# MLP up-projection of a hybrid encoder block as seven block products (Strassen) with 256-column moving tiles

## The chip, the cores and the metric

One core of one Trainium2 chip runs the whole block in one launch. The metric is device time in microseconds, from the first to the last instruction of an execution; lower is better. Engines are named as in the profile: PE (matmul), PEld (its weight loads), DVE, ACT, POOL, SP (which issues nearly all DMAs).

## What is computed

One layer with 512 tokens of width 2048. The change touches one product in its second half:

```
h  = x + W_out( sig(gA) * P_A(NAtt(xn)) + sig(gB) * P_B(BiGDN(xn)) ),  xn = RMSNorm(x)
h  = h + W_down( relu(RMSNorm(h) W_up)^2 )        # W_up 2048 x 8192, W_down 8192 x 2048
y  = RMSNorm_final(h)
```

All data are float32. Tokens stand on the free axis (T = 512), channels on the 128 partitions, so the product with W_up has 64 output tiles of 128 channels, each summed over 16 tiles of 128 input channels.

## The kernel before

**Precision by splitting.** A matmul takes rounded operands (float32r). Each operand is therefore kept as a high half, a rounded copy made on ACT (`S_.copy`, L89 and L94), and a low half, what the rounding lost, made on DVE by a subtraction (L90 and L95). A product of two tiles is three matmuls, high by high, high by low and low by high (L115 to L117, `unit_mm`), each with a weight load of its own.

**Weights.** W_up lies in DRAM as units `wup[m, u]` of 128 x 1024 floats (512 KB): output tile m, half u of the input channels, eight 128 x 128 blocks. `load_unit` (L85) loads one (tag `raw`, four buffers), casts it (`wh`, three buffers) and subtracts (`wl`, three buffers). One unit feeds 24 matmuls.

**Stages at the change.** Around it the kernel runs, one after the other on PE:

- L795 to L815: the projections of both branches and their gated sum `mix`, 32 tiles (high and low) in the pool `bp` (tag `B`, 48 buffers of 128 x 512).
- L849 to L864: W_out, 16 output tiles of 48 matmuls. Each result is added to x (L855), stored to `hTD` for later (L856), scaled by the norm's weights and split into `hh[m]`, `hl[m]` (L861, L862). The first eight pairs go to `bp`, the other eight to the pool `hq` on the right-hand side of memory (L858, L860). `sumsq` gathers squares for the norm.
- L865: the task `stat("h")` makes the row of reciprocal roots `rB`. Tasks advance when `pump()` is called inside `unit_mm`, every four channel tiles; it puts some tiny matmuls between the others.
- L867 to L874: the up-projection. For each m of 64, 2 x 24 matmuls of 512 columns into one bank; u = 0 reads `hh[0..7]`, u = 1 reads `hh[8..15]`. DVE applies relu and `rB` (L872), ACT squares (L873), SP stores to `hidD[m]` (L874).
- L875, L876: while m >= 40, eleven of the first sixteen hidden tiles are already loaded back and split (`load_hid`, L841).
- L878 to L896: the down-projection in four blocks of 16 hidden tiles, added into `Ha` (loaded from `hTD` at L882); its last two output tiles are done in halves of 256 columns (L918 to L934), 192 matmuls.

PSUM holds seven banks for these stages (L785) and one for statistics. Pools on the right-hand side form a stack: one that is opened after another was closed gets the same place, and with `reuse_waits="tile"` a tile waits for just those tiles that it overwrites.

**What sets the order.** The text gives priorities and dependencies. When the program is built, a list scheduler picks for each engine the ready instruction of highest priority, so an engine's order is not that of the text, but it is fixed from then on, and each engine and each DMA queue runs its own list in order, waiting where a semaphore isn't there yet.

```
def unit_mm(ps, unit, rhs, k0, first, last, view=None):
    hi, lo = unit
    for kk in range(8):
        rh, rl = rhs[k0 + kk]
        w = slice(kk * 128, (kk + 1) * 128)
        PE.matmul(ps, hi[:, w], rh, start=first and kk == 0, stop=False)
        PE.matmul(ps, hi[:, w], rl, start=False, stop=False)
        PE.matmul(ps, lo[:, w], rh, start=False, stop=last and kk == 7)
```

Of the kernel before, what the change touches and what calls it, by code (L numbers as in the profile page):

```python
# [19 lines left out]
T = 512  # L20
# [7 lines left out]
NPUMP = 4  # L28
# [21 lines left out]
def tile_hybrid_block(  # L50
# [17 lines left out]
    nlw_s = cp.tile([128, KX], F32, name="nlw_s")  # L68
# [5 lines left out]
    def big(name, dt=F32R):  # L74
        return bp.tile([128, T], dt, tag="B", name=name)

    def ev(name):
        return st.tile([128, T], F32, tag="ev", name=name, bufs=4)

    def load_raw(src, name):  # L80
        raw = st.tile([128, 1024], F32, tag="raw", name=f"raw_{name}", bufs=4)
        nc.sync.dma_start(out=raw, in_=src)
        return raw

    def load_unit(src, name):  # L85
# [15 lines left out]
    def pump():  # L101
        for t in list(tasks):
            try:
                next(t)
            except StopIteration:
                tasks.remove(t)
# [5 lines that stand above are left out]
            if view is not None:  # L112
                rh, rl = view(rh), view(rl)
# [4 lines that stand above are left out]
            if kk % NPUMP == NPUMP - 1:  # L118
                pump()
# [31 lines left out]
    rB = cp.tile([128, T], F32, tag="rB", name="rB")  # L151
# [24 lines left out]
    hidD = dp.tile([64, 128, T], F32, name="hidD")  # L176
# [4 lines left out]
    X = []  # L181
    with ExitStack() as p0:
# [128 lines left out]
        for r in (127, 0):  # L311
            t = dn.tile([128, 128], F32, name=f"sel{r}")
# [411 lines left out]
        i = 3  # L724
# [40 lines left out]
        for h in range(NH):  # L765
            qkv = []
            for e, kind in enumerate(("aq", "ak", "av")):
                ps = mtile((kind, h), perm)
                t = ap.tile([128, T], F32, tag=kind, name=f"{kind}{h}", bufs=1 if e < 2 else 2)
# [5 lines left out]
            t = att_task(h, *qkv, ap)  # L775
# [8 lines left out]
    with ExitStack() as p1:  # L784
# [3 lines left out]
        def bank():  # L788
            return mmp.tile([128, T], F32, tag="mm", name="ps_b")

        mix = []
        with ExitStack() as p4:
# [3 lines left out]
            for h in range(NH):  # L796
                raw = ev(f"ybr{h}")
# [43 lines left out]
        def load_hid(k):  # L841
            raw = ev(f"hr{k}")
            nc.sync.dma_start(out=raw, in_=hidD[k])
            return split(raw, big(f"hih{k}"), big(f"hil{k}"))

        hT = []
        with ExitStack() as p5:
            hq = p5.enter_context(tc.tile_pool(name="hq", bufs=1, side="right", reuse_waits="tile"))
            for m in range(16):  # L849
                ps = bank()  # L850
                xr = ev(f"xr{m}")
                nc.sync.dma_start(out=xr, in_=xT[:, m, :])
                for u in range(2):
                    unit_mm(ps, load_unit(wout[m, u], f"wo{m}_{u}"), mix, 8 * u, u == 0, u == 1)
                V.tensor_tensor(out=xr, in0=ps, in1=xr, op=ALU.add)  # L855
                nc.sync.dma_start(out=hTD[m], in_=xr)  # L856
                if m < 8:
                    hh, hl = big(f"hh{m}"), big(f"hl{m}")  # L858
                else:
                    hh, hl = hq.tile([128, T], F32R, name=f"hh{m}"), hq.tile([128, T], F32R, name=f"hl{m}")  # L860
                S_.activation(out=hh, in_=xr, func=AF.Copy, scale=nlw_s[:, m : m + 1])  # L861
                V.scalar_tensor_tensor(out=hl, in0=xr, scalar=nlw_s[:, m : m + 1], in1=hh.bitcast(F32), op0=ALU.mult, op1=ALU.subtract)  # L862
                hT.append((hh, hl))
                sq = sumsq(xr, m, f"h{m}")  # L864
            tasks.append(stat("h", sq))  # L865
            hid0 = []
            for m in range(64):  # L867
                ps = bank()
                for u in range(2):
                    unit_mm(ps, load_unit(wup[m, u], f"up{m}_{u}"), hT, 8 * u, u == 0, u == 1)  # L870
                r = ev(f"ur{m}")
                V.scalar_tensor_tensor(out=r, in0=ps, scalar=0.0, in1=rB, op0=ALU.max, op1=ALU.mult)  # L872
                S_.activation(out=r, in_=r, func=AF.Square)  # L873
                nc.sync.dma_start(out=hidD[m], in_=r)  # L874
                if m >= 40 and m % 2 == 1 and len(hid0) < 11:  # L875
                    hid0.append(load_hid(len(hid0)))  # L876

        hp = p1.enter_context(tc.tile_pool(name="hp", bufs=1, side="right", reuse_waits="tile"))  # L878
        Ha = hp.tile([128, 16, T], F32, name="Ha")
# [4 lines left out]
        for b in range(NB):  # L884
# [4 lines left out]
            for m in range(14 if last else 16):  # L889
                ps = bank()  # L890
# [22 lines left out]
        for m in (14, 15):  # L913
            for u in range(2):
                raw = load_raw(wdn[m, 2 * NB - 2 + u], f"dnl{m}_{u}")
                for e in range(2):
                    pieces[m, 2 * u + e] = split(raw[:, e * T : (e + 1) * T], big(f"wlh{m}{u}{e}"), big(f"wll{m}{u}{e}"))
        for half in range(2):  # L918
            ts = slice(half * 256, half * 256 + 256)
            for m in (14, 15):  # L920
                ps = bank()[:, 0:256]
                for k in range(16):
                    wh, wl = pieces[m, k // 4]
                    w = slice(k % 4 * 128, k % 4 * 128 + 128)
# [7 lines left out]
                sq = sumsq(H[m], m, f"f{m}_{half}", ts)  # L932
# [88 lines left out]
```

## Time and profile before

| | us |
|---|---|
| median of 2 runs | 2957.06 |
| lowest, highest run | 2955.55, 2958.57 |
| profiled execution: span | 2960.0 |
| of it W_out (from the first to the last start) | 1360.36 to 1534.23 |
| of it the up-projection | 1534.46 to 2244.15 |
| PE busy | 2913.1 |
| DVE busy | 1365.7 |
| ACT busy | 872.6 |

The profiled execution is given by its span; no other time stands on its page. A busy time counts an engine's instructions from their start to their (for matmuls modelled) end. Matmuls overlap, so the distance between their starts tells what one costs PE. "Idle before" is the time that the engine sat idle ahead of a group of instructions, with what ended it.

### The profile page before, as it was taken

Reading aid. Unit: us, or ns where it says so; the run is one execution under the profiler, and the core shown is the slowest. Engines: PE = TensorE matmul, PEld = TensorE weight load, DVE = VectorE, ACT = ScalarE, POOL = GpSimd, SP = SyncE. Lnnn points to the kernel's source line nnn. Section 1 sums busy time; section 2 is a strip of 40 time slices with the busy share of each in tenths; the row PEclk is TensorE's granted clock in tenths of the full one; section 3 lists DMA queues with packets and bytes.
Section 4 is the critical chain, followed back from the end, with each engine's and each line's share of the span. In section 5 each row is a group of like instructions: output and inputs, shape, how many; then the busy total and the mean of one; then the engine's idle time right before and its main releaser. Section 6 shows DMA issues by size and latency. Waiting matters only on the chain.

```text
span 2960.0 us, 33906 instructions
## 1 busy us (share of the span) xinstructions
PE 2913.1 (98%) x13432; PEld 2397.5 (81%) x13432; DVE 1365.7 (46%) x2071; ACT 872.6 (29%) x1333; POOL 24.7 (1%) x66
## 2 busy tenths in 40 slices
PE   8999999999999999999999999999999999999998
PEld 6778788888788888888888888888888888888887
DVE  6888769744554443444342222223333242332333
ACT  6444322233233333222222222222223131221322
POOL 0000000000000000000000000000000000000000
PEclk9999999999999999999999999999999999999999
DMA  7556653655532223443433333334336243342322
GB/s 228 185 182 186 207 185 118 219 153 171 183 114 96 91 85 132 160 155 117 148 125 114 123 119 118 120 118 136 128 129 230 94 155 100 107 143 94 113 100 86
DMA packets 170847, 411.95 MB, mean 139 GB/s; under 512 B 34368, under 2 KB 46720, under 8 KB 170688
## 3 DMA queue, kind: packets, MB, share of 16 engines
q1 hardware_dynamic: 170016, 407.69, 41.7%
q0 software_dynamic: 672, 2.10, 0.3%
q8 instruction: 105, 1.72, 0.2%
q14 instruction: 54, 0.44, 0.0%
HBM read 350.84 MB, written 58.88 MB: 138 GB/s over the span
## 4 chain that ended last, share of the span: by engine, by line
PE 72%; DVE 0%; SPq 0%; DMA 0%; ACT 0%; issue 0%; DVEq 0%; POOL 0%
PE ps_b L115 20%; PE ps_b L116 20%; PE ps_b L117 20%; PE ps_mm L117 4%; PE ps_mm L115 3%; PE ps_mm L116 3%; PE ps_ax L676 0%; PE ps_b L926 0%; PE ps_b L927 0%; PE ps_b L928 0%; DVE Ha L906 0%; PE ps_ax L137 0%; PE ps_ax L690 0%; PE ps_ax L692 0%; PE ps_ax L691 0%; PE ps_ax L657 0%
## 5 line engine op out<-in xcount | busy, mean ns | idle before, releaser
L115 PE MATMUL ps_mm<-xh,wh_in 128*128 128x512 f32 x1416 | 567.3, 401 | 3.4 <-ACT wh_in L89 3.4
L117 PE MATMUL ps_mm<-xh,wl_in 128*128 128x512 f32 x1416 | 560.6, 396 | 1.3 <-DVE wl_in L90 1.3
L116 PE MATMUL ps_mm<-xl,wh_in 128*128 128x512 f32 x1416 | 560.0, 395 | 0.0
L115 PE MATMUL ps_b<-hh,wh_up 128*128 128x512 f32 x1024 | 402.0, 393 | 0.0
L117 PE MATMUL ps_b<-hh,wl_up 128*128 128x512 f32 x1024 | 401.7, 392 | 0.0
L116 PE MATMUL ps_b<-hl,wh_up 128*128 128x512 f32 x1024 | 401.5, 392 | 0.0
L116 PE MATMUL ps_b<-hil,wh_dn 128*128 128x512 f32 x992 | 385.8, 389 | 0.0
L117 PE MATMUL ps_b<-hih,wl_dn 128*128 128x512 f32 x992 | 385.7, 389 | 0.0
L115 PE MATMUL ps_b<-hih,wh_dn 128*128 128x512 f32 x992 | 385.7, 389 | 0.0
L117 PEld LDWEIGHTS ps_mm<-xh,wl_in 128*128 128x128 f32 x1416 | 267.8, 189 | 62.3 <-DVE wl_in L90 2.6
L115 PEld LDWEIGHTS ps_mm<-xh,wh_in 128*128 128x128 f32 x1416 | 267.7, 189 | 59.1 <-ACT wh_in L89 4.0
L116 PEld LDWEIGHTS ps_mm<-xl,wh_in 128*128 128x128 f32 x1416 | 267.8, 189 | 54.7 <-issue 0.2
L89 ACT CAST wh_in<-raw_in 128x1024 fp32r<-128x1024 f32 x177 | 186.0, 1051 | 414.5 <-PE ps_mm L116 325.7
L89 ACT CAST wh_up<-raw_up 128x1024 fp32r<-128x1024 f32 x128 | 134.6, 1052 | 529.1 <-PE ps_b L116 300.0
L90 DVE TENSOR_TENSOR wl_up<-raw_up,wh_up 128x1024 fp32r<-128x1024 f32 x128 | 156.8, 1225 | 274.5 <-ACT wh_up L89 274.5
L90 DVE TENSOR_TENSOR wl_in<-raw_in,wh_in 128x1024 fp32r<-128x1024 f32 x177 | 216.2, 1222 | 121.4 <-ACT wh_in L89 114.8
L89 ACT CAST wh_dn<-raw_dn 128x1024 fp32r<-128x1024 f32 x124 | 130.9, 1055 | 477.1 <-PE ps_b L116 461.5
L90 DVE TENSOR_TENSOR wl_dn<-raw_dn,wh_dn 128x1024 fp32r<-128x1024 f32 x124 | 151.9, 1225 | 244.4 <-ACT wh_dn L89 244.1
L116 PEld LDWEIGHTS ps_b<-hl,wh_up 128*128 128x128 f32 x1024 | 192.2, 188 | 43.8 <-issue 0.2
L115 PEld LDWEIGHTS ps_b<-hh,wh_up 128*128 128x128 f32 x1024 | 192.2, 188 | 43.6 <-issue 0.2
L117 PEld LDWEIGHTS ps_b<-hh,wl_up 128*128 128x128 f32 x1024 | 192.1, 188 | 43.4
L116 PEld LDWEIGHTS ps_b<-hil,wh_dn 128*128 128x128 f32 x992 | 186.2, 188 | 38.9 <-DVE hil L95 0.2
(307 smaller groups left out, 3203.1 us busy)
## 6 DMA issues: line engine op xcount, KB each, us to landing
raw_in<-in_win SPq DMA_DIRECT2D x177, 512.0 KB
raw_up<-in_wup SPq DMA_DIRECT2D x128, 512.0 KB
raw_dn<-in_wdn SPq DMA_DIRECT2D x124, 512.0 KB
raw_wo<-in_wout SPq DMA_DIRECT2D x32, 512.0 KB
hidD<-ur SPq DMA_DIRECT2D x64, 256.0 KB
hr<-hidD SPq DMA_DIRECT2D x64, 256.0 KB
gD<-g SPq DMA_DIRECT2D x32, 256.0 KB
raw_pa<-in_wpa SPq DMA_DIRECT2D x16, 512.0 KB
```

The lines of the kernel that those rows point to most:

```text
L89: S_.copy(out=hi, in_=raw)
L90: V.tensor_tensor(out=lo, in0=raw, in1=hi.bitcast(F32), op=ALU.subtract)
L115: PE.matmul(ps, hi[:, w], rh, start=first and kk == 0, stop=False)
L116: PE.matmul(ps, hi[:, w], rl, start=False, stop=False)
L117: PE.matmul(ps, lo[:, w], rh, start=False, stop=last and kk == 7)
```

## The change

The up-projection is cut in two along output tiles, input channels and tokens. With A the weights (A11 = `wup[m0, 0]`, A12 = `wup[m0, 1]`, A21 = `wup[m1, 0]`, A22 = `wup[m1, 1]`, m1 = m0 + 8) and X the normed input (first index: input channels 0 to 7 or 8 to 15; second: tokens 0 to 255 or 256 to 511), a round makes the output tiles m0 and m1 from seven products instead of eight. There are 32 rounds. Each product is 8 x 3 matmuls of 256 columns.

- Weight sums: S1 = A21 + A22 and S3 = A21 + A11 are each made by a load on SP and an accumulating DMA on POOL (`accum_op=ALU.add`), S2 = S1 + A11 and S4 = S2 + A12 by additions on DVE. The scheme takes the lower row of A with the opposite sign, so that all four are additions; the tiles m1 come out negated, so a minimum stands ahead of their square where m0 has a maximum.
- Operand sums: T1 to T4 by four operations on DVE per pair of W_out tiles (`tr` pool, 8 buffers), split at the end of W_out into `bp`. X11 goes to a new right-hand pool `bq`. W_out runs its tiles in the order 0, 8, 1, 9, and so on.
- Partial results meet in three banks a, b and c per round, which are read by ACT and DVE between two products; t1, t5 and u2 hold 256 columns each.
- The first round has another order of products: those with X11, X22 and X21 first.
- The first sixteen hidden tiles are loaded after the last round instead of eleven within the stage.

```
+        p7 = ExitStack()
+        bq = p7.enter_context(tc.tile_pool(name="bq", bufs=8, side="right", reuse_waits="tile"))
+
+        def operand(src, name):
+            t = bq.tile([128, T], F32R, tag="B2", name=name) if name.startswith("X11") else big(name)
+            return split(src, t[:, 0:256], t[:, 256:512])
...
-            for m in range(16):
+            tr = p5.enter_context(tc.tile_pool(name="tr", bufs=8, side="right", reuse_waits="tile"))
+            for n, m in enumerate(m for j in range(8) for m in (j, j + 8)):
...
+                sq = sumsq(xr, n, f"h{m}")
+                S_.activation(out=xr, in_=xr, func=AF.Copy, scale=nlw_s[:, m : m + 1])
+                xs.append(xr)
+                if n % 2 == 0:
+                    XS["11", m] = operand(xr[:, lo_t], f"X11_{m}")
                 else:
+                    j = n // 2
+                    x0, x1 = xs[n - 1], xs[n]
+                    XS["21", j] = operand(x1[:, lo_t], f"X21_{j}")
+                    XS["22", j] = operand(x1[:, hi_t], f"X22_{j}")
+                    t = tr.tile([128, 4, 256], F32, tag="tr", name=f"TR{j}")
+                    V.tensor_tensor(out=t[:, 0], in0=x0[:, lo_t], in1=x0[:, hi_t], op=ALU.subtract)
+                    V.scalar_tensor_tensor(out=t[:, 1], in0=t[:, 0], scalar=-1.0, in1=x1[:, hi_t], op0=ALU.mult, op1=ALU.subtract)
+                    V.tensor_tensor(out=t[:, 2], in0=x1[:, hi_t], in1=x0[:, hi_t], op=ALU.subtract)
+                    V.scalar_tensor_tensor(out=t[:, 3], in0=t[:, 1], scalar=-1.0, in1=x1[:, lo_t], op0=ALU.mult, op1=ALU.subtract)
             tasks.append(stat("h", sq))
-            hid0 = []
-            for m in range(64):
-                ps = bank()
-                for u in range(2):
-                    unit_mm(ps, load_unit(wup[m, u], f"up{m}_{u}"), hT, 8 * u, u == 0, u == 1)
...
+            for o, e in (("T2", 1), ("T1", 0), ("T3", 2), ("T4", 3)):
+                for j in range(8):
+                    XS[o, j] = operand(TR[j][:, e], f"X{o}_{j}")
+        with ExitStack() as p6:
+            sm = p6.enter_context(tc.tile_pool(name="sm", bufs=1, side="right", reuse_waits="tile"))
+            def sums(name, bufs=4):
+                return sm.tile([128, 1024], F32, tag="sum", name=name, bufs=bufs)
...
+            def product(ps, w, o, first=False):
+                hi, lo = w
+                for j in range(8):
+                    rh, rl = XS[o, j]
+                    c = slice(j * 128, (j + 1) * 128)
+                    PE.matmul(ps, hi[:, c], rh, start=first and j == 0, stop=False, skip_group_check=True)
+                    PE.matmul(ps, hi[:, c], rl, start=False, stop=False, skip_group_check=True)
+                    PE.matmul(ps, lo[:, c], rh, start=False, stop=j == 7, skip_group_check=True)
...
+            for i in range(32):
+                m0 = i // 8 * 16 + i % 8
+                m1 = m0 + 8
+                a11 = load_raw(wup[m0, 0], f"A11_{i}")
+                s1, s3 = sums(f"S1_{i}"), sums(f"S3_{i}")
+                nc.sync.dma_start(out=s1, in_=wup[m1, 0])
+                G.dma_start(out=s1, in_=wup[m1, 1], accum_op=ALU.add)
+                a12 = load_raw(wup[m0, 1], f"A12_{i}")
+                nc.sync.dma_start(out=s3, in_=wup[m1, 0])
+                G.dma_start(out=s3, in_=wup[m0, 0], accum_op=ALU.add)
+                a22 = load_raw(wup[m1, 1], f"A22_{i}")
+                a, b, c = (bank()[:, 0:256] for _ in range(3))
...
+                s2, s4 = sums(f"S2_{i}"), sums(f"S4_{i}")
+                product(a, wsplit(a11, f"A11_{i}"), "11", True)
+                S_.copy(out=t1, in_=a)
+                V.tensor_tensor(out=s2, in0=s1, in1=a11, op=ALU.add)
+                if i == 0:
+                    V.tensor_tensor(out=s4, in0=s2, in1=a12, op=ALU.add)
+                    product(c, wsplit(s4, f"S4_{i}"), "22", True)
+                    S_.copy(out=t5, in_=c)
+                    product(a, wsplit(a12, f"A12_{i}"), "21")
+                product(b, wsplit(s2, f"S2_{i}"), "T2", True)
+                V.tensor_tensor(out=u2, in0=b, in1=t1, op=ALU.add)
+                product(c, wsplit(s1, f"S1_{i}"), "T1", i > 0)
...
+                    S_.copy(out=t5, in_=c)
+                    product(a, wsplit(a12, f"A12_{i}"), "21")
+                V.scalar_tensor_tensor(out=r0[:, lo_t], in0=a, scalar=0.0, in1=rB[:, lo_t], op0=ALU.max, op1=ALU.mult)
+                product(b, wsplit(s3, f"S3_{i}"), "T3")
+                V.tensor_tensor(out=t5, in0=b, in1=t5, op=ALU.add)
+                V.tensor_tensor(out=t5, in0=t5, in1=t1, op=ALU.add)
+                V.scalar_tensor_tensor(out=r1[:, hi_t], in0=t5, scalar=0.0, in1=rB[:, hi_t], op0=ALU.min, op1=ALU.mult)
+                if i > 0:
+                    V.tensor_tensor(out=s4, in0=s2, in1=a12, op=ALU.add)
+                    product(c, wsplit(s4, f"S4_{i}"), "22")
+                V.tensor_tensor(out=u2, in0=c, in1=u2, op=ALU.add)
+                V.scalar_tensor_tensor(out=r0[:, hi_t], in0=u2, scalar=0.0, in1=rB[:, hi_t], op0=ALU.max, op1=ALU.mult)
+                S_.activation(out=r0, in_=r0, func=AF.Square)
+                nc.sync.dma_start(out=hidD[m0], in_=r0)
+                product(b, wsplit(a22, f"A22_{i}"), "T4")
+                V.tensor_tensor(out=t1, in0=b, in1=t1, op=ALU.add)
+                V.scalar_tensor_tensor(out=r1[:, lo_t], in0=t1, scalar=0.0, in1=rB[:, lo_t], op0=ALU.min, op1=ALU.mult)
+                S_.activation(out=r1, in_=r1, func=AF.Square)
+                nc.sync.dma_start(out=hidD[m1], in_=r1)
+            hid0 = [load_hid(k) for k in range(16)]
+        p7.close()
```

## Rows read from the trace of the kernel before

**Rows 1.** The page: span, busy time of PE, and its granted clock by slices.
```profile
span 2960.0 us, 33906 instructions
PE 2913.1 (98%) x13432; PEld 2397.5 (81%) x13432; DVE 1365.7 (46%) x2071; ACT 872.6 (29%) x1333; POOL 24.7 (1%) x66
...
PEclk9999999999999999999999999999999999999999
```

**Rows 2.** Waits of PE, 1183 to 2950 us, the longest: total, times, longest.
```profile
PE ps_b L149 <- DVE dg_f L145: 2.9, 1, 2.9
```

**Rows 3.** Timeline of PE: first matmul of the up-projection, last two halves, next stage's first.
```profile
1534.46 0.39 PE L115 MATMUL ps_b<-hh,wh_up 128*128 128x512 f32 x1
...
2234.71 0.39 PE L116 MATMUL ps_b<-hl,wh_up 128*128 128x512 f32 x1
...
2238.34 0.39 PE L117 MATMUL ps_b<-hh,wl_up 128*128 128x512 f32 x1
2238.56 0.40 PE L115 MATMUL ps_b<-hh,wh_up 128*128 128x512 f32 x1
...
2244.15 0.39 PE L115 MATMUL ps_b<-hih,wh_dn 128*128 128x512 f32 x1
```

**Rows 4.** Busy times of the up-projection: PE, PEld, DVE, ACT, POOL, PEclk, DMA share, GB/s.
```profile
1534.46:2244.15 709.69, 709.69 (x3091) 578.73 (x3090) 211.26 (x217) 175.81 (x205) 0.00 (x0) 1.00 0.37 123
```

**Rows 5.** Timeline of PE and PEld: the 256-column matmuls of the last output tiles.
```profile
2919.01 0.28 PE L926 MATMUL ps_b<-hih,wlh 128*128 128x256 f32 x1
2919.02 0.19 PEld L927 LDWEIGHTS ps_b<-hil,wlh 128*128 128x128 f32 x1
...
2934.73 0.28 PE L928 MATMUL ps_b<-hih,wll 128*128 128x256 f32 x1
```

**Rows 6.** Groups of DVE and ACT: 1550 to 2245 us, then whole-run rows by form.
```profile
L90 DVE TENSOR_TENSOR wl_up<-raw_up,wh_up 128x1024 fp32r<-128x1024 f32 x123 | 150.7, 1225 | 266.0 <-ACT wh_up L89 266.0
L89 ACT CAST wh_up<-raw_up 128x1024 fp32r<-128x1024 f32 x123 | 129.4, 1052 | 507.5 <-PE ps_b L116 286.7 <-issue 220.8
L873 ACT ACTIVATE ur<-ur 128x512 f32<-128x512 f32 x63 | 39.3, 624 | 1.3 <-DVE ur L872 1.3
...
L453 DVE SCALAR_TENSOR_TENSOR bB<-ps_ax,bB 128x256 f32<-128x256 f32 x32 | 12.7, 420 | 2.3 <-PE ps_ax L443 2.2
L590 ACT COPY vn<-ps_ax 128x256 f32<-128x256 f32 x32 | 11.5, 373 | 25.4 <-PE ps_ax L589 25.0
L94 ACT CAST ph<-ps_ax 128x256 fp32r<-128x256 f32 x16 | 6.0, 377 | 0.0
```

**Rows 7.** A lone load of 512 KB: SP's issues, then busy times by microsecond.
```profile
1804.64 5.79 SPq L82 DMA_DIRECT2D raw_up<-in_wup  x2
...
1812.00:1813.00 1.00, 1.00 (x6) 0.82 (x5) 0.00 (x0) 0.00 (x0) 0.00 (x0) 1.00 0.76 311
1813.00:1814.00 1.00, 1.00 (x6) 0.81 (x5) 0.47 (x1) 0.65 (x1) 0.00 (x0) 1.00 0.02 8
```

**Rows 8.** DMAs from POOL, 512 KB each: issue; time to landing; engines' share meanwhile (last two figures).
```profile
L466 POOL DMA_DIRECT2D MT<-Nd x2: 1050/1050/1050, 373.3 to 374.4; - x2
DMA to landing us min/median/max: 11.5/12.7/14.0
376.00:381.00 5.00, 5.00 (x24) 4.14 (x23) 2.52 (x3) 1.58 (x2) 1.34 (x3) 1.00 0.98 296
```

**Rows 9.** Busy times of the W_out stage, columns as in rows 4.
```profile
1360.00:1534.46 174.46, 174.46 (x772) 144.42 (x771) 70.19 (x80) 51.46 (x63) 0.00 (x0) 1.00 0.41 138
```

**Rows 10.** Timeline of DVE around the end of W_out.
```profile
1524.68 1.23 DVE L90 TENSOR_TENSOR wl_up<-raw_up,wh_up 128x1024 fp32r<-128x1024 f32 x1 [0.21 <-ACT wh_up L89]
...
1534.66 0.69 DVE L855 TENSOR_TENSOR xr<-ps_b,xr 128x512 f32<-128x512 f32 x1 [3.31 <-PE ps_b L117]
```

**Rows 11.** Timeline at the start of the down-projection: SP's late hidden loads, first addition.
```profile
2255.21 2.34 SPq L843 DMA_DIRECT2D hr<-hidD  x4
...
2267.55 0.69 DVE L893 TENSOR_TENSOR Ha<-ps_b,Ha 128x512 f32<-128x512 f32 x1 [1.58 <-PE ps_b L117]
```

More of the change, by code (lines that the diff above doesn't have):

```diff
@@ L844, in load_hid @@
             return split(raw, big(f"hih{k}"), big(f"hil{k}"))
-        hT = []
+        p7 = ExitStack()
[3 more added lines that the diff above has]
+            return split(src, t[:, 0:256], t[:, 256:512])
+        lo_t, hi_t = slice(0, 256), slice(256, 512)
+        XS = {}
         with ExitStack() as p5:
-            hq = p5.enter_context(tc.tile_pool(name="hq", bufs=1, side="right", reuse_waits="tile"))
-            for m in range(16):
+            tr = p5.enter_context(tc.tile_pool(name="tr", bufs=8, side="right", reuse_waits="tile"))
+            TR = []
+            xs = []
+            for n, m in enumerate(m for j in range(8) for m in (j, j + 8)):
                 ps = bank()
@@ L856, in tile_hybrid_block @@
                 nc.sync.dma_start(out=hTD[m], in_=xr)
-                if m < 8:
-                    hh, hl = big(f"hh{m}"), big(f"hl{m}")
-                else:
[L860 to L863, printed above, removed]
@@ L864, in tile_hybrid_block @@
-                sq = sumsq(xr, m, f"h{m}")
-            tasks.append(stat("h", sq))
-            hid0 = []
-            for m in range(64):
-                ps = bank()
-                for u in range(2):
-                    unit_mm(ps, load_unit(wup[m, u], f"up{m}_{u}"), hT, 8 * u, u == 0, u == 1)
[L871 to L876, printed above, removed]
+                sq = sumsq(xr, n, f"h{m}")
@@ new lines, in tile_hybrid_block @@
+                S_.activation(out=xr, in_=xr, func=AF.Copy, scale=nlw_s[:, m : m + 1])
+                xs.append(xr)
+                if n % 2 == 0:
+                    XS["11", m] = operand(xr[:, lo_t], f"X11_{m}")
+                else:
+                    j = n // 2
[7 more added lines that the diff above has]
+                    V.scalar_tensor_tensor(out=t[:, 3], in0=t[:, 1], scalar=-1.0, in1=x1[:, lo_t], op0=ALU.mult, op1=ALU.subtract)
+                    TR.append(t)
@@ new lines, in tile_hybrid_block, with et, wsplit @@
+            tasks.append(stat("h", sq))
+            for o, e in (("T2", 1), ("T1", 0), ("T3", 2), ("T4", 3)):
[5 more added lines that the diff above has]
+                return sm.tile([128, 1024], F32, tag="sum", name=name, bufs=bufs)
+            def et(name):
+                return sm.tile([128, 256], F32, tag="et", name=name, bufs=6)
+            def wsplit(raw, name):
+                hi = st.tile([128, 1024], F32R, tag="wh", name=f"wh_{name}", bufs=3)
+                lo = st.tile([128, 1024], F32R, tag="wl", name=f"wl_{name}", bufs=3)
+                return split(raw, hi, lo)
+            def product(ps, w, o, first=False):
[6 more added lines that the diff above has]
+                    PE.matmul(ps, lo[:, c], rh, start=False, stop=j == 7, skip_group_check=True)
+                    if j % NPUMP == NPUMP - 1:
+                        pump()
+            for i in range(32):
[10 more added lines that the diff above has]
+                a, b, c = (bank()[:, 0:256] for _ in range(3))
+                t1, t5, u2 = et(f"t1_{i}"), et(f"t5_{i}"), et(f"u2_{i}")
+                r0, r1 = ev(f"ur{m0}"), ev(f"ur{m1}")
+                s2, s4 = sums(f"S2_{i}"), sums(f"S4_{i}")
[10 more added lines that the diff above has]
+                product(c, wsplit(s1, f"S1_{i}"), "T1", i > 0)
+                if i == 0:
+                    V.tensor_tensor(out=t5, in0=c, in1=t5, op=ALU.subtract)
+                else:
+                    S_.copy(out=t5, in_=c)
[18 more added lines that the diff above has]
+            hid0 = [load_hid(k) for k in range(16)]
```

## The prediction

> **What bounds the kernel now.** I read the page from the top. TensorE is busy 98% of a span of 2960.0 us, at full granted clock in all 40 slices [rows 1]. That alone proves little, because a pipelined matmul is shown longer than its share of the array: the rows say 392 ns each, and yet one starts every 227 ns. So I looked at what PE waits for: from the branch projections to the end its longest wait is 2.9 us, for the row `dg_f` of the final norm, and none falls into the MLP up-projection, where PE is busy for all of it [rows 2, 4]. The stage is therefore worth its number of matmuls times the distance between their starts. It runs from 1534.46 to 2244.15 us, 709.7 us [rows 3]. Its 64 tiles have two halves: where the moving tile is one of the first eight `hh`/`hl`, 16 starts lie in 3.63 us, 226.9 ns each; with the eight in the right-hand pool, 24 in 5.59 us, 232.9 ns [rows 3]. 1536 x 0.2269 + 1536 x 0.2329 = 706.2; the statistics of the norm take the other 3.5.
>
> DVE is busy 211 us and ACT 176 us of these 709.7, and the DMA engines 0.37 of their time at 123 GB/s [rows 4]. So all but PE have room, and the stage shrinks only if its columns or the fixed cost per matmul do.
>
> **What it removes and adds on PE.** Removed: 64 x 48 = 3072 matmuls of 512 columns. Added: 32 x 7 x 24 = 5376 of 256 columns. The columns fall to 7/8, but the number of matmuls rises to 7/4, so everything hangs on what a 256-column matmul costs. The kernel has such a stretch: at its end, 131 distances between 2919.01 and 2934.73 give 120.0 ns each, every matmul with a weight load of its own of 0.19 us beside it [rows 5]. Two of them cost 240 ns against 226.9 for one of 512: 13 ns are paid per matmul, not per column. 5376 x 0.1200 = 645.1 us. The eight X11 operands lie in a right-hand pool, as the slower half did; 6 ns for 768 matmuls is 4.6 us (bounds 0 and 4.6; I take 4.6, the same place in memory). With the statistics, 645.1 + 4.6 + 3.5 = 653.2: 56.5 us less than now. Seven eighths of 706.2 would have given 88; the halved tile eats a third of that.
>
> In a loop that streams 256 columns, the Trainium skill ("TensorE: Matmul & The Clock Gate", Back-to-back issue gap) gives 262 cycles at 2.4 GHz, an estimate of 109 ns, by which the 5376 would take 587 us. The row says 120.0, and at 512 columns the same section's 518 cycles are 216 ns where the rows show 226.9, so the rows decide.
>
> **Beside PE, per block row.** One of the 32 rounds lasts 168 x 0.120 = 20.2 us. DVE: seven low halves of 1024 columns at 1.225, two sums of the same shape (s2, s4; nearest row the same subtraction) 2 x 1.23, nine operations on 256 columns at 0.42 [rows 6]: 8.6 + 2.5 + 3.8 = 14.9, 74%. ACT: seven casts at 1.05, two copies at 0.37, two squares at 0.62: 9.3, 46%. Both fit. Three `wh`/`wl` buffers mean that a unit may be split once the third one before it is done, 2 x 2.88 = 5.8 us ahead of its product; cast, hand-over and subtraction take 1.05 + 0.2 + 1.23 = 2.5, so each low half has 3.3 us of slack for queueing on DVE. An engine's order is not that of the text: today DVE makes low halves of the up-projection before it has added the last W_out tile [rows 10]. The evacuations between two products on one bank have a product or more (2.88 us) to pass in; b before T4 is tightest, one 0.42 addition in one product. I put 2 us in all on these (0 to 10).
>
> **The sums by DMA.** Per round SP loads five pieces of 512 KB instead of four in 22 us, and POOL adds two more; stores stay at two of 256 KB. That is 4.2 MB in 20.2 us, 208 GB/s; at 123 GB/s for 0.37 of the engines, a share of 0.63. The chain that matters is that of S1: its buffer is free after its split; load; accumulation; s2 and split. A lone load of 512 KB is issued at 1810.10 (the second in the 5.79 us from 1804.64, whose issue ends 1810.43) and the engines are quiet again by 1813: 3.0 us [rows 7]. No accumulating DMA is in this trace. Bounds: 3.0, a plain load, and 14.0, the slowest 512-KB DMA from POOL, whose pieces are short and which met full engines [rows 8]. I take 7: rows of 4 KB as in the plain load, plus POOL's 1.05 us of issue and twice the transfer. The four sum buffers serve one round, so the chain closes on itself: sum of S1 and split some 3.5, load 3.0, accumulation L, or L + 6.5 against 20.2 us. Up to L of about 13.5 PE does not wait. At 7 the chain has 6.7 us to spare.
>
> The trace has no price for an accumulation; "Collectives: The Full Stack" in the Trainium skill (The bandwidth ceiling) says that an adding DMA costs its second source read, not the addition. By that rule the two accumulations would load the engines like four loads, an estimated 260 GB/s or 0.79 of the engines; no row here shows it.
>
> **The stage before.** W_out keeps its PE work. DVE gains 56 low halves and 32 differences of 256 columns, 88 x 0.42 = 37, and loses sixteen low halves of 512; it is busy 70 of 174.5 us there, ACT 51 and gains 56 x 0.38 = 21 [rows 6, 9]. Hidden, but for the end. The `sm` pool stands where `tr` stood, so S1 to S4 of the first round can't be loaded before the differences they overwrite are split for the last time, and those splits take the `B` buffers of `mix`, the last free only as W_out ends. Now the last W_out tile leaves PE at 1534.46, and its addition, with the work on it to follow, begins at 1534.66 [rows 3, 10]. With the backlog of 32 T splits (13 us of DVE, about half before the end), S1 begins some 3 us after the end, lands 3 + 7 later, and takes 2.3 for s2 and its cast: 15. PE has A11, A12 and perhaps the next A11, 5.8 to 8.6 us. I take a gap of 8, bounds 0 and 20.
>
> **The stage after.** Eleven hidden tiles used to be split before the down-projection began; now all 16 loads stand behind the last round, need the operands' buffers, and meet the 16 loads of Ha on SP. Five late ones already stood behind Ha today: issued from 2255.21, while PE went on with other output tiles, the first Ha addition coming only at 2267.55 [rows 11], 23 us after the start instead of 11, and PE did not wait. So late tiles of the second half cost nothing, late tiles of the first half do. I take 4, bounds 0 and 12.
>
> **Sum.** 653.2 + 2 + 8 + 4 = 667.2 against 709.7: 42.5 us less. The span is 2.9 us above the median of the runs, 0.1%, which I leave out: 2957.06 - 42.5 = 2914.6, call it 2915. With all three small terms at their ends, and X11 at 0 on the lower side: 648.6 to 695.2, so 2896 to 2943.
>
> **Rivals.**
> (a) The accumulation is the new bound (slower than before). If one takes longer than 13.5 us each round waits for L - 13.5, 31 times. It eats the gain from L of 14.9 on (1.4 x 31 = 43); at 18 it costs 140 and the time is 3055. For it: the only 512-KB DMAs from POOL took 11.5 to 14.0 [rows 8]. Against it: those were made of short pieces and ran while the engines were full.
> (b) DVE becomes the bound by its order: if each low half waits for its own cast with nothing in between (today 266 us of such waits stand before 123 of them [rows 6]), a round costs 14.9 + 7 x 1.25 = 23.7 us, 32 x 23.7 = 757, plus 3.5 and 12: 773, 63 more than now, 3020. Against it: DVE does not run in text order, and other work is there.
> (c) The two hand-overs are not covered: 20 at the start, 12 at the end, 10 in the rounds: 2943. For it: the overwritten `tr` pool, the late hidden tiles. Against: only once per kernel.
> (d) The 13 ns per matmul belong to the last stretch, not to short tiles, and 256 columns cost half of 512: 113.4 ns [rows 3]. 5376 x 0.1134 = 609.9, with 4.6 + 3.5 + 14 makes 632, 78 less: 2879. Against it: 131 starts in a row show 120.0, and both kinds of matmul fit the same 13 ns. By the 109 ns of the Trainium skill's section named above this rival would end at about 2856.
>
> **How the numbers follow.** Forecast 0.65, (a) 0.10, (b) 0.06, (c) 0.15, (d) 0.04. The range 2896 to 2965 holds the forecast with its own bounds and (c), and a mild (a); left out are (d) and most of (a) and (b), under 0.2. A measurement of this kernel can tell about 2% from no change, 59 us. The forecast's best end, 61 less, barely gets there: faster 0.04 + 0.03. Slower by over 2%: most of (a), half of (b), 0.11. Within 2%: 0.82.
>
> **What would show it.** Right: starts of 256-column matmuls 120 ns apart in the middle of the stage, rounds of 20.2 to 20.5 us, no PE wait on `wl` of a sum, one gap of several us after W_out. (a) shows as PE, ACT and DVE waiting for the DMA into S1 or S3 each round, and landings over 13 us. (b) shows as DVE above 90% and PE waiting for DVE. (c) is read from the first round and the first down-projection tiles. If the distance of starts in mid-stage isn't 120 ns, the main term is wrong, and nothing else in the sum can make up for it: 5 ns are 27 us.

## The result, and the profile after

The changed kernel takes 3001.49 us (median of 2 runs, 2996.19 to 3006.78) against 2957.06: a ratio of 1.0149, interval 1.0104 to 1.0193. The prediction said 2915, in a range of 2896 to 2965. It has the sign wrong and lies 86 us off.

The profiled execution, 34.4 us longer than that of before (2994.4 against 2960.0), shows where. The page of the changed kernel answers to [rows 1]: PE's share is down, and one slice has a lower clock.

```profile
span 2994.4 us, 39661 instructions
PE 2874.6 (96%) x15736; PEld 2474.7 (83%) x15736; DVE 1637.0 (55%) x2528; ACT 1014.8 (34%) x1549; POOL 80.8 (3%) x130
...
PEclk9999999999999999999979999999999999999999
```

PE's own work did shrink: 2913.1 to 2874.6 us busy. The up-projection, from the first 256-column matmul at 1529.72 to the first of the down-projection at 2272.62, lasts 742.9 us where it lasted 709.7 [rows 3]. Where [rows 2] had nothing in this stage, PE's longest waits now are these (total, times, longest):

```profile
PE ps_b L909 <- DVE wl_S L95: 35.7, 29, 2.3
PE ps_b L907 <- ACT wh_S L94: 27.9, 1, 27.9
PE ps_b L907 <- DVE t L946: 6.6, 26, 0.3
```

One is a single gap at the start, the others come in every round. Against [rows 4], PE stands still in both stretches (busy times by window; columns as there):

```profile
1529.80:1562.50 32.70, 4.75 (x42) 4.55 (x40) 18.25 (x54) 13.46 (x39) 1.85 (x2) 0.59 0.35 84
1608.70:2231.60 622.90, 582.15 (x4707) 572.30 (x4706) 393.76 (x505) 253.22 (x309) 48.90 (x56) 0.99 0.71 190
```

**The rounds.** The store of a round's first tile marks each round on SP; the first and the last of 29:

```profile
1608.22 0.33 SPq L955 DMA_DIRECT2D hidD<-ur  x1
...
2231.03 0.45 SPq L955 DMA_DIRECT2D hidD<-ur  x1
```

(2231.03 - 1608.22) / 28 = 22.24 us a round. Starts of matmuls are 0.120 us apart wherever PE runs, so 168 of them take 20.1. Of the missing 2.1 us some 1.6 stand at one place of the round; 0.35 stand ahead of the product with T4, whose bank DVE empties late behind the same instructions, and 0.2 in short stretches at half the clock (last section). PE's timeline has, at that one place, two matmuls of S4 with its high half, and then the first that needs its low half:

```profile
1910.11 0.28 PE L908 MATMUL ps_b<-X,wh_S 128*128 128x256 f32 x1
1912.68 0.39 PE L909 MATMUL ps_b<-X,wl_S 128*128 128x256 f32 x1 [2.29 <-DVE wl_S L95]
```

S4's cast was done by 1905.4. DVE's timeline shows why its low half was not:

```profile
1902.56 1.23 DVE L95 TENSOR_TENSOR wl_S<-S,wh_S 128x1024 fp32r<-128x1024 f32 x1 [0.51 <-ACT wh_S L94]
1910.26 1.23 DVE L930 TENSOR_TENSOR S<-S,raw_A 128x1024 f32<-128x1024 f32 x1 [6.48 <-DMA S<-in_wup]
1911.41 1.22 DVE L95 TENSOR_TENSOR wl_S<-S,wh_S 128x1024 fp32r<-128x1024 f32 x1
```

Between 1903.8 and 1910.26 DVE does nothing. The next instruction of its list is the sum S2 of the *next* round, which waits for that round's accumulating DMA; the low half of S4 (1911.41) stands behind it.

**The loop behind the wait.** One round later the whole cycle can be followed. SP's timeline has the load of S1, of this round and of the next, each issued when the low half of a sum has given a buffer back:

```profile
1919.69 0.33 SPq L918 DMA_DIRECT2D S<-in_wup  x1
...
1942.07 0.86 SPq L918 DMA_DIRECT2D S<-in_wup  x1
```

POOL's timeline has the accumulation, issued when that load has landed:

```profile
1925.51 0.88 POOL L919 DMA_DIRECT2D S<-in_wup  x1 [20.13 <-DVE u L937]
```

DVE's has S2, when the accumulation has landed, and the low half (to 1942.04) whose end lets the next load go:

```profile
1932.64 1.23 DVE L930 TENSOR_TENSOR S<-S,raw_A 128x1024 f32<-128x1024 f32 x1 [5.70 <-DMA S<-in_wup]
...
1940.82 1.22 DVE L95 TENSOR_TENSOR wl_S<-S,wh_S 128x1024 fp32r<-128x1024 f32 x1
```

Load 5.8, accumulation 7.1, DVE from S2 to that low half 9.4: 22.4 us from one load to the next, and that is the round. In the 28 rounds the three parts are 6.1 (5.6 to 6.8), 6.7 (5.7 to 7.9) and 9.4 us in the mean, 22.2 together, and in each of these rounds DVE waits for the accumulation ahead of S2: the loop has no slack anywhere. (A releaser is inferred: POOL's issue is put down to an operation of DVE, but what its instruction waits for is the load. On SP the load also stands right behind the store L955, issued 0.47 us before it, so with SP's list as it is a buffer that came free earlier should hardly help; no run tests that alone.)

**The start.** The chain of work that ended last, where PE stands still, in order of time:

```profile
1537.89 10.74 DVE XT L95 x32
1548.74 3.95 DMA S<-in_wup
1552.71 6.05 DMA S<-in_wup
1558.86 1.24 DVE S L930
1560.11 1.24 DVE S L932
1561.37 1.05 ACT wh_S L94
```

All 32 splits of the T's come behind W_out's end, and the load of S1, issued at 1548.32, behind the last but one of them. Distances of more than 0.30 us between starts, less the usual 0.12 of each, add up to 30.0 us here.

**The end.** From the first down-projection matmul to the end of the span: 721.8 us, before 715.9.

So 34.4 = 33.2 in the stage + 5.9 behind it - 4.7 ahead of it (W_out began earlier in this execution).

### The profile page after: what moved, and what is told of

Same layout as the page of the kernel before. It is cut to its first block, busy times and chain, and to the rows that moved or that the text cites. A ratio compares the mean times of both kernels' runs of the same rounds, so it can differ in the third digit from the quotient of the medians.

```text
span 2994.4 us, 39661 instructions
## 1 busy us (share of the span) xinstructions
PE 2874.6 (96%) x15736; PEld 2474.7 (83%) x15736; DVE 1637.0 (55%) x2528; ACT 1014.8 (34%) x1549; POOL 80.8 (3%) x130
## 4 chain that ended last, share of the span: by engine, by line
PE 71%; DMA 14%; DVE 10%; issue 3%; ACT 1%; SPq 0%; DVEq 0%; POOLq 0%; ACTq 0%
PE ps_b L115 11%; PE ps_b L117 11%; PE ps_b L116 11%; DMA S<-in_wup 9%; PE ps_mm L115 8%; PE ps_mm L116 8%; PE ps_mm L117 8%; PE ps_b L907 3%; PE ps_b L909 3%; PE ps_b L908 3%; DVE wl_S L95 2%; DVE wl_A L95 2%; DMA bB<-rowD 1%; DVE wl_in L90 1%; DMA Nd<-bB 1%
## 5 line engine op out<-in xcount | busy, mean ns | idle before, releaser
L115 PEld LDWEIGHTS ps_b<-hih,wh_dn 128*128 128x128 f32 x992 | 186.2, 188 | 42.5 <-ACT hih L94 3.4
L907 PE MATMUL ps_b<-XT,wh_S 128*128 128x256 f32 x768 | 218.0, 284 | 2.4 <-DVE u L937 2.4
L117 PEld LDWEIGHTS ps_b<-hih,wl_dn 128*128 128x128 f32 x992 | 186.3, 188 | 39.9 <-DVE wl_dn L90 2.0
L909 PE MATMUL ps_b<-XT,wl_S 128*128 128x256 f32 x768 | 218.1, 284 | 0.0
L908 PE MATMUL ps_b<-XT,wh_S 128*128 128x256 f32 x768 | 217.9, 284 | 0.0
L94 ACT CAST wh_S<-S 128x1024 fp32r<-128x1024 f32 x128 | 133.7, 1045 | 233.1 <-PE ps_b L908 165.8
L95 DVE TENSOR_TENSOR wl_S<-S,wh_S 128x1024 fp32r<-128x1024 f32 x128 | 156.2, 1220 | 22.5 <-ACT wh_S L94 21.9
L907 PEld LDWEIGHTS ps_b<-XT,wh_S 128*128 128x128 f32 x768 | 148.0, 193 | 2.5 <-issue 2.5
```

The lines of the kernel that those rows point to most:

```text
L907: PE.matmul(ps, hi[:, c], rh, start=first and j == 0, stop=False, skip_group_check=True)
L908: PE.matmul(ps, hi[:, c], rl, start=False, stop=False, skip_group_check=True)
L909: PE.matmul(ps, lo[:, c], rh, start=False, stop=j == 7, skip_group_check=True)
```

## The experiments

Each run was timed beside the kernel before on the same chip; the ratio is to that. "Rounds" is the mean over 27 or 28 rounds, "gap" the sum of PE's distances over 0.30 us, less 0.12 of each, in the first 50 us of the stage, "stage" from the first 256-column matmul to the first of the down-projection, from each run's profile. In the first three rows and in runs 4 to 6 the gap holds 1.8 to 3.6 us of later waits; without them the changed kernel has the 30.0 us from above, runs 1 and 2 have 29.1 and 29.3, runs 4 to 6 22.8, 14.3 and 10.9.

| run | us | ratio, interval | rounds | gap | stage |
|---|---|---|---|---|---|
| changed kernel | 3001.49 | 1.0149, 1.0104 to 1.0193 | 22.24 | 32.5 | 742.9 |
| e1_order | 2943.49 | 0.9953, 0.9936 to 0.9969 | 20.56 | 32.7 | 693.4 |
| e2_bufs6 | 2942.62 | 0.9956, 0.9938 to 0.9973 | 20.37 | 31.1 | 687.8 |
| e3_noacc | 2923.10 | 0.9885, 0.9867 to 0.9904 | 20.13 | 23.0 | 670.7 |
| e4_start | 2977.29 | 1.0070, 1.0045 to 1.0095 | 22.10 | 25.3 | 729.4 |
| e5_start2 | 2968.17 | 1.0042, 1.0029 to 1.0055 | 21.91 | 16.1 | 718.1 |
| e6_combo | 2929.25 | 0.9907, 0.9892 to 0.9922 | 20.46 | 13.1 | 674.1 |
| e7_dvesum | 2922.89 | 0.9889, 0.9874 to 0.9904 | 20.13 | 24.7 | 671.3 |
| e8_poolsum | 2928.56 | 0.9905, 0.9890 to 0.9919 | 20.09 | 26.9 | 673.5 |
| e9_best | 2915.84 | 0.9860, 0.9844 to 0.9876 | 20.13 | 12.1 | 661.2 |
| e10_end | 2911.97 | 0.9848, 0.9833 to 0.9862 | 20.13 | 12.5 | 660.7 |

**1. DVE's order alone.**

```
+                with tc.issue_after(low[f"S4_{i - 1}"].ins) if i > 0 else nullcontext():
                     V.tensor_tensor(out=s2, in0=s1, in1=a11, op=ALU.add)
```

> The only edit: DVE's addition for S2 of a round is queued behind the low half of S4 of the round before; all else, the four sum buffers and the accumulating DMAs too, stays. Theory (order): a round lasts 22.3 us instead of 20.2 because DVE stands at the next round's S2, waiting for the accumulating DMA (176 us in all), while the low half of S4, whose cast has long been done, is queued behind it and PE waits for it (2.6 us a round). With the two swapped PE's wait for that low half is gone, rounds are 20.2 to 20.6 us, 31 x 1.9 = 59 us less: about 2940 us, 0.993 of the kernel before; DVE still waits for the DMA, at no cost. Rival 1 (the chain through the four buffers itself is too long: free buffer, load, accumulation, sum, split): the wait comes up at S2's own low half instead, rounds stay above 21.8 us, 2985 to 3001 us. Rival 2 (DVE has too much to do): no change, 2995 to 3005 us.

Measured: the waits for a sum's low half are gone from PE's list, rounds of 20.56 us, 2943.49 us. The order theory's forecast came true: the medians lie 58 us apart, of 59 expected, and the stage of the profiled execution is 50 us shorter. What is left is a short wait for the evacuation ahead of T4, in half of the rounds (PE's waits of this run, columns as above):

```profile
PE ps_b L911 <- ACT wh_S L902: 27.1, 1, 27.1
PE ps_b L911 <- DVE t L951: 8.5, 15, 0.9
```

DVE still waits for the DMA, 79.0 us instead of 176.2 (its waits):

```profile
DVE S L935 <- DMA S<-in_wup: 79.0, 32, 9.4
```

The rounds still scatter, from 19.5 to 21.4 us, where those of runs 3 and 7 below take 20.12 or 20.13 from the second on to the last but one. So rival 1 was not wholly wrong: the edit takes one low half out from between S2 and the low half that frees the buffer (8.0 us instead of 9.4 at 1908.12), and load, accumulation and DVE's part, 5.6 + 7.0 + 8.0 us in the mean of 28 rounds, still add up to the round. The loop still sets it; it has become shorter, and hardly longer than PE's own work.

**2. Six buffers for the sums.**

```
-            def sums(name, bufs=4):
+            def sums(name, bufs=6):
```

> The only edit: six buffers for the sums instead of four, so that a load of S1 or S3 waits for a buffer that was given back most of a round earlier; the builder's scheduler then also puts S2 of the next round some 10 us earlier in DVE's order. Theory (order) and rival 1 (chain) both say that DVE's wait for the DMA goes: rounds of 20.2 to 20.6 us, about 2940 us, 0.993 of the kernel before. Rival 2 (DVE has too much to do, 14.9 of 20.2 us, in a bad order): rounds stay at 22 us, 2990 to 3001 us. Rival 3 (the DMA engines can't carry 208 GB/s beside the accumulation): landings grow beyond 9 us as the loads crowd together and rounds stay above 21 us.

Measured: 2942.62 us, and PE's waits for a sum's low half down to 6.2 us in seven places. Rounds are 20.37 us: six buffers do as much as the other order. They also change DVE's order, though: in this run S2 of the next round stands behind the low half of S4 too (1912.53 and 1898.33), so it can't tell the loop from the order. Landings of the accumulations grew to 8.8 us (5.6 to 10.8) from 7.1, towards rival 3's 9, and the rounds did not.

**3. Without the accumulations.** The accumulations into S1 and S3 are left out, so the tiles computed with these two sums are not the product.

```
-                G.dma_start(out=s1, in_=wup[m1, 1], accum_op=ALU.add)
-                G.dma_start(out=s3, in_=wup[m0, 0], accum_op=ALU.add)
```

> The two accumulating DMAs are left out (S1 and S3 are A21 alone); every addition, split and matmul remains. It prices the accumulation and nothing else. Theory (order) and rival 1 (chain): some 7 us come off the wait for S1, so DVE is no longer held: rounds of 20.2 to 20.5 us, and the gap at the start, 29.5 us, loses the 6 us of its accumulation: 2930 to 2936 us, 0.991 of the kernel before. Rival 2 (DVE too busy): rounds stay at 22 us, 2990 us or more.

Measured: 20.13 us each round from the second on to the last but one, and PE busy for all of the middle of the stage (busy times, columns as in [rows 4]):

```profile
1600.00:2100.00 500.00, 500.00 (x4175) 500.00 (x4175) 365.55 (x449) 225.71 (x273) 0.00 (x0) 1.00 0.48 157
```

The time, 2923.10 us, is below the 2930 to 2936 expected. This confirms the main term: 32 x 20.13 = 644.2, predicted 645.1. The rest of the stage's 670.7 is the gap, 23.0 (one accumulation shorter), and the statistics.

**4 and 5. The start.** Run 4 splits the T's of pairs 0 to 3 (`tsplit` makes the four splits of each pair that it is given) behind the first half of the last W_out tile:

```
+                    if n == 15 and u == 0:
+                        tsplit(range(4))
```

> The only edit is at the hand-over from W_out: sixteen of the 32 splits of T1 to T4 (channel pairs 0 to 3, pair by pair) are put behind the first half of the last W_out tile, the other sixteen behind its end, where all 32 stood operand by operand. Theory: the 29.5 us gap of PE is the chain last W_out matmul, T splits (10.8 us on DVE), load and accumulation of the first S1 (about 10.5 us, its memory is that of the T's first pair), S2, S4 and cast (4 us). With the first pairs split some 5 us before W_out's end, S1's load starts about 15 us earlier: a gap of 10 to 16 us and 2981 to 2988 us for the whole, rounds unchanged at 22.3 us. Rival (the gap is set by X21 and X22 of the last tile or by the statistics, not by the memory under S1): the gap stays above 25 us, 2996 to 3001 us.

Run 5 differs in the pairs only, `tsplit((6, 5, 3, 2))`.

> Like the run before it at the hand-over (16 of the 32 splits behind the first half of the last W_out tile), but with those channel pairs first whose memory the first sums take: S1 lies over the T's of pairs 5 and 6, S3 over 2 and 3, where the earlier run had split pairs 0 to 3 first and S1's load had still waited for pair 6, until 1539.7. Theory (the gap is the wait for the memory under S1 and what follows): S1's load is issued near 1525, in front of W_out's end, lands with its accumulation some 10 us later, S2, S4 and the cast take 3.7: the first S4 product starts near 1540, a gap of 5 to 10 us instead of 29.5, rounds unchanged near 22 us, 2974 to 2982 us. Rival (S1's load is held by SP's queue or by DVE's work on the last tile): the gap stays near 21 us, 2982 to 2990 us.

Measured: 2977.29 and 2968.17 us, both below their ranges, although the gaps, 22.8 and 14.3 us without the later waits, are longer than the 10 to 16 and 5 to 10 expected. (Both ranges were reckoned from 3001.49, a median of two runs 10.6 us apart; by the profiled executions the stage is 13.5 and 24.8 us shorter.) What S1's load waits for is in SP's timeline. That of run 4:

```profile
1539.71 0.33 SPq L924 DMA_DIRECT2D S<-in_wup  x1
```

That of run 5:

```profile
1517.75 11.21 SPq L874 DMA_DIRECT2D hTD<-xr  x2
1529.05 0.38 SPq L924 DMA_DIRECT2D S<-in_wup  x1
```

In run 4 it is the memory: S1 lies over the T's of pairs 5 and 6, which that run splits in its second half. In run 5 those are free near 1525, but SP stands until 1529 at the store of the last W_out tile (L874), and the load is queued behind it; that was the rival's mechanism. These 4 us are not what PE waits for in that run, though. S1's accumulation, issued at 1533.31, has landed after 5.3 us, and DVE comes to S2 only behind the sixteen splits that were left:

```profile
1535.80 5.45 DVE L95 TENSOR_TENSOR XT<-TR,XT 128x256 fp32r<-128x256 f32 x16
1541.17 1.22 DVE L936 TENSOR_TENSOR S<-S,raw_A 128x1024 f32<-128x1024 f32 x1
```

Rounds hardly changed, as expected. The two runs show that the gap and the rounds are separate losses.

**6. Both together**, with A12 by X21 ahead of S4 by X22 in the first round.

> Three edits together: S2 behind the low half of S4 of the round before (first run), the pairs under the first sums split first (run before this one), and in the first round the product A12 by X21, which needs no sum, ahead of S4 by X22. Theory: rounds of 20.4 us, gap at the start of 2 to 7 us in pieces, about 6 us at the end; 2943 less 22: 2916 to 2925 us, 0.986 to 0.990 of the kernel before, so nearly all of the 42 us of the prediction. Rival (the two losses aren't independent, for instance because an early start only moves the wait to the second round): above 2932 us.

Measured: 2929.25 us, a little above the 2916 to 2925 expected and below the rival's 2932. The gap is still 13.1 us, where 2 to 7 were expected, the rounds 20.46. This is the changed kernel in its own form, with most of its two losses mended: faster than before by 0.9%.

**7 and 8. The sums without accumulating DMAs**, by additions on DVE (run 7) or on POOL (run 8, `G` in place of `V`):

```
-                nc.sync.dma_start(out=s1, in_=wup[m1, 0])
-                G.dma_start(out=s1, in_=wup[m1, 1], accum_op=ALU.add)
+                a21 = sm.tile([128, 1024], F32, tag="a21", name=f"A21_{i}", bufs=2)
+                nc.sync.dma_start(out=a21, in_=wup[m1, 0])
+                a22 = load_raw(wup[m1, 1], f"A22_{i}")
+                V.tensor_tensor(out=s1, in0=a21, in1=a22, op=ALU.add)
...
+                V.tensor_tensor(out=s3, in0=a21, in1=a11, op=ALU.add)
```

> S1 and S3 by additions on DVE from a loaded A21 (two buffers of its own) instead of accumulating DMAs; A22 is loaded once, ahead of A12. Three pieces of 512 KB fewer per round move; DVE gets 2 x 1.23 us more, 17.4 of 20.2 us. Theory (the accumulating DMA's latency, not the bytes or DVE's load, made the rounds long): DVE no longer waits for a DMA that takes 13 us from its issue on SP, rounds of 20.2 to 20.8 us, gap at the start 6 us shorter: 2922 to 2942 us. Rival (DVE is near its limit, its order decides): at 17.4 us and the waits for casts rounds are 21.5 us or more, 2965 us or more.

> S1 and S3 by additions on POOL from a loaded A21, else like the run before. A POOL operation on 256 columns took 0.73 us in the kernel before, so one on 1024 should take 2.9 and POOL be busy 5.8 of 20.2 us. Theory: rounds of 20.2 to 20.6 us and 2925 to 2940 us; DVE 55% as before. Rival (POOL's additions slow DVE's down beside them): DVE's 1024-column operations grow from 1.22 us by a tenth or more, and rounds stay above 21 us, 2955 us or more.

Measured, run 7: 2922.89 us, inside the 2922 to 2942 expected, rounds of 20.13 us, PE without a wait from the first gap to the end of the stage, DVE at 83% beside it:

```profile
1600.00:2100.00 500.00, 500.00 (x4176) 500.00 (x4175) 416.28 (x498) 226.27 (x274) 0.00 (x0) 1.00 0.39 132
```

The busier DVE is the better one: it waits for nothing that takes 13 us. Run 8, 2928.56 us of 2925 to 2940 expected, also keeps PE fed, but its rival was right on the slowing. DVE's low halves, 1.22 us in run 7, are longer beside POOL's additions (groups of DVE in run 8, 1600 to 2180 us; each a mean over those that meet POOL and those that don't):

```profile
L95 DVE TENSOR_TENSOR wl_S<-S,wh_S 128x1024 fp32r<-128x1024 f32 x116 | 177.5, 1530 | 17.9 <-ACT wh_S L94 17.3
L95 DVE TENSOR_TENSOR wl_A<-raw_A,wh_A 128x1024 fp32r<-128x1024 f32 x87 | 126.6, 1455 | 44.1 <-ACT wh_A L94 44.1
```

POOL's two additions in the same stretch:

```profile
L923 POOL TENSOR_TENSOR S<-A,raw_A 128x1024 f32<-128x1024 f32 x29 | 98.3, 3390 | 1.2 <-DVE wl_S L95 1.2
L921 POOL TENSOR_TENSOR S<-A,raw_A 128x1024 f32<-128x1024 f32 x29 | 72.1, 2485 | 412.8 <-DMA raw_A<-in_wup 300.1 <-DVE wl_S L95 100.1 <-DVE ur L958 12.6
```

**9 and 10. Run 7 with its start mended, then the end too.** Run 9's splits begin with the pairs under the first tiles, the last `hTD` store goes out on POOL's queue, and buffers are set so that no early tile lies over the last pair:

```
+                        tsplit((6, 1, 5, 2))
...
+                (G if n == 15 else nc.sync).dma_start(out=hTD[m], in_=xr)
```

> The version with S1 and S3 added on DVE, and its start mended: the pairs of T under A21, t1, S1 and S3 are split behind the first half of the last W_out tile, the store of that tile's hTD goes out on POOL's queue instead of SP's (on SP the first sum's load had stood behind it until W_out's end, at 1529), A21 has one buffer and the small partial results four, so that nothing early lies over the last pair; A12 by X21 stands ahead of S4 by X22 in the first round, and the norm's broadcast matmul waits for two more pumps. Theory (rounds are at PE's pace, 20.16 us; only the start gap of 23 us was left): A21 loads from about 1525, S4's cast ends near 1539, and what is left is the wait for the copy of t1, queued on ACT behind the splits: 4 to 8 us of gaps. 2923 less 15 to 19: 2903 to 2909 us, 0.982 to 0.985 of the kernel before. Rival (one buffer for A21 or four for the partial results close a new loop): rounds above 20.4 us, 2915 us or more.

Run 10 adds:

```
+                raw = sums(f"hr{k}")[:, 0:T]
```

> The run before it, with one edit at the end of the stage: the first sixteen hidden tiles are loaded into the buffers of the sums, free during the last round, instead of the four buffers that the last round's results still use. Theory: the first loads go out some 8 us earlier and PE's small waits at the start of the down-projection, about 2 us in named waits, go: 1 to 5 us less than the run before it. Rival (the operands' buffers, which come free one product after another, set these loads): no difference beyond 1 us.

Measured: 2915.84 us for run 9, above its range. It is not the rival's new loop, since rounds are 20.13 us. PE waits 5.5 us for the copy of t1, which was expected, and 4.1 us for the cast of S4. A21 was there in time, but the sums were not: on DVE they stood behind sixteen late splits, as S2 did in run 5. The last ten of them, on the chain of what ended last:

```profile
1543.54 3.43 DVE XT L95 x10
1546.97 1.14 DVE S L928
```

Run 10: 2911.97 us, 3.9 less than run 9, inside its 1 to 5; behind the stage PE has 717.3 us to the end of the span, 5 fewer than in run 9 (722.3). This is the fastest version that was run: 1.5% below the kernel before, with the interval given above.

## Why the prediction was wrong

**The main term was right.** Starts 120 ns apart as in [rows 5], rounds of 20.13 us as soon as nothing holds them, 644 us against 645.1. Rival (d) is out. The 4.6 us for X11 were not there: its operands lie in a right-hand pool, and yet starts in that product are 0.12 us apart too (1920.92, 1921.04, 1921.15, 1921.27). So the 6 ns of [rows 3] don't follow that place in memory to 256 columns; what makes them at 512 no run shows.

**The step that failed is the loop of the sums**: "The four sum buffers serve one round, so the chain closes on itself: sum of S1 and split some 3.5, load 3.0, accumulation L, or L + 6.5 against 20.2 us". L itself was put at 7 and measured 7.1 (the landings of the page; 5.7 to 8.6 in the middle of the stage). The other two terms were mis-sized, both in the same way: a price of the operation alone was taken for its time in the queue.
- The load was 3.0, from a lone load on quiet engines [rows 7]. In the round it is issued between two stores and another piece, with the engines at 0.71, and took 5.8 (6.1 in the mean). Which of these makes it longer no run tells apart.
- Sum and split were 3.5, as if DVE had nothing else to do. But from S2 to the low half that gives the buffer back stand twelve instructions on DVE, both counted, 9.4 us without idle time.

With these the limit for L is 20.1 - 5.8 - 9.4 = 4.9 us, not 13.5, and L - 4.9 = 2.2 us a round is what rounds of 22.24 are missing (2.1). Rival (a)'s mechanism, "the accumulation is the new bound", came true at half of its threshold. Its sign (DVE waiting for the DMA into a sum) was named; the sign that PE would not wait "on `wl` of a sum" is what failed. Run 3 takes L out, and the rounds are PE's own 20.13. Run 1 takes one low half out of DVE's part, and the rounds are the shorter loop, 20.56. These two runs and the sum of the three parts in every round are why I call the loop shown; run 2 fits, but changes DVE's order as well. It is not the amount that the DMA engines carry: run 1 moves the same pieces, in shorter rounds.

**"Each low half has 3.3 us of slack for queueing on DVE"** failed with it. The slack was reckoned against DVE's own work. The thing that queued ahead of S4's low half was not work but a wait, 6.48 us of it, and DVE is 63% busy (393.76 of 622.90) in a stage that it bounds. Rival (b), DVE bound by its order with each low half waiting for its own cast, is not what happened: those waits, 40.5 us for the `wl_A`, cost PE nothing. Rival (b) asked for DVE above 90%; a queue can bind without that.

**Start: 8 us predicted (0 to 20), 30.0 measured.** The step was "With the backlog of 32 T splits (13 us of DVE, about half before the end)". None was before the end. The parts behind it were near: S1 "lands 3 + 7 later" took 4.0 + 6.1, s2, s4 and the cast 3.6. Rival (c) had the place, and 20 for the price. What lengthens it and I didn't look for is the norm's statistics and the last tile's own operands on DVE ahead of the splits (from 1533 to 1537.8). SP's queue adds nothing here: SP had come to S1's load 17 us before it could issue it.

**End: 4 us predicted (0 to 12), 5.9 measured.** Right in place and size; run 10 takes 5 of it away.

**Sum.** 644 + 30 + 65 (31 rounds by 2.1) = 739 of the 743 measured; of the other 4, a later wait in the first round takes 2.5, and the rest is left for the statistics. Of the forecast's 42.5 us gain, the rounds took 65 and the start 22 more than allowed for.

**The DMA engines.** I had put their share at 0.63 for rounds of 20.2 us by bytes alone. At 20.5 us a round (run 6, 1700 to 2100 us) it is 0.75 at 205 GB/s. Run 3, without the accumulations, shows 0.48 at 157, and run 7, without one more load, 0.39 at 132: by these differences 0.09 for a load and 0.13 for an accumulation. The queues of run 6 tell it more directly (its DMAs from 1700 to 2100 us: packets, MB, share of the 16 engines; q0 has the accumulations alone, q1 the loads and stores):

```profile
q1 hardware_dynamic: 19309, 60.36, 44.7%
q0 software_dynamic: 5754, 20.95, 29.5%
```

Per MB the accumulations take 1.41% against 0.74%, 1.9 times as much, so 0.15 for one of them. "Collectives: The Full Stack" in the Trainium skill (The bandwidth ceiling) says that an adding DMA costs its second source read. The trace agrees: 1.9 is near the 2 of the rule, and 0.75 near the estimate of 0.79 by it.

## What to carry to other kernels

When a few buffers close a loop through a DMA and an engine, add up the loop with the times *in their queues*, not with the price of each operation alone: everything that stands on that engine between taking the data and giving the buffer back is part of it. An in-order engine that is 60% busy can still bound a kernel, because one instruction that waits for a DMA holds up the ready ones behind it; look for what the waiting instruction stands in front of. And where an addition would take an engine 1.2 us, an accumulating DMA that lands after 7 isn't free merely because that engine looks busy: here two more additions on DVE, with the start as it was, came out no slower than the accumulations with start and order mended (2922.89 against 2929.25).

## What was not expected of the hardware

- The 6 ns by which matmuls with a moving tile in the right-hand pool are slower at 512 columns [rows 3] are absent at 256 (changed kernel, product with X11).
- POOL additions on 1024 columns took 2.5 and 3.4 us and stretched DVE's low halves of the same shape that ran beside them to 2.23 and 2.68 us (run 8, 1707.64 and 1710.55), from 1.22; an operation that reads a PSUM bank kept its 0.41 beside the same addition (1709.80). The accumulating DMAs from POOL, 0.88 us of issue each, left DVE's 1.22 as it was.
- After the long gap PE's granted clock is 0.50 for some 3.5 us (1562.50 to 1565.50), 1.2 GHz of its 2.4; starts are up to 1.0 us apart there, and 0.21 just before they come back to 0.12 at 1566. It makes the 28.2 us of standing still into 30.0. The clock had fallen to 0.50 at 1535.5, while PE stood still. It fell for a short while five more times in this stage (at 1580, 1648, 1867, 2024 and 2181), each time behind a wait of PE of over 2 us; starts are 0.21 apart there. Run 3 has none of these five, and none of these waits. The busy times of the first stretch, columns as in [rows 4]:

```profile
1562.50:1565.50 3.00, 3.00 (x8) 1.97 (x9) 3.00 (x3) 2.30 (x3) 0.00 (x0) 0.50 0.36 97
```
